# A hybrid decoder layer on one core: one block's convolution as diagonal matrices on TensorE, and the scan's scalings of x made for all chunks at once

## The chip, the core and the metric

The program runs on one core of a Trainium2 chip. The engines are named as in the profile: PE (TensorE matmul; PEld is its weight load), DVE (VectorE), ACT (ScalarE), POOL (GpSimd) and SP (SyncE, which issues most DMAs). The metric is the device time of one execution in microseconds (us): the median of three runs before the change is 1674.62 us (1671.99 to 1677.26). Everything is computed in float32 or in the matmul type fp32r; a product that has to be exact is made of three fp32r matmuls (high by high, high by low, low by high).

## The reference, cut to what matters

528 tokens (16 learned meta tokens and 512 of the sequence) with 1024 features pass one layer. The part that is touched is the mixing sub-layer:

```
u    = rmsnorm(h, norm_mix_w)
z, xbc, dt_raw, conf_in = split(u @ w_in)
# SSD group: conv of width 4, silu, then a chunked scan, 16 heads in 4 groups, chunks of 128 tokens
xdt    = xh * dt
y_diag = (C B^T * exp(segsum(dt*A))) @ xdt          # inside a chunk
states = B^T @ (decay * xdt)                        # carried from chunk to chunk
y      = y_diag + C @ prev_state * exp(cumsum) + D * xh
y      = rmsnorm_per_group(y * silu(z)) * ssd_norm_w
# Conformer group: GLU, causal depthwise conv of width 31, LayerNorm over 1024 channels, swish
g      = a * sigmoid(gate)                          # 1024 channels
hc[t]  = sum_j g[t + j - 30] * conv_w[j] + conv_b   # each channel by itself
yc     = silu(layernorm(hc) * ln_g + ln_b)
h      = h + concat(y, yc) @ w_out                  # 2048 x 1024
```

After it comes the channel sub-layer (a product-key retrieval over 128 x 128 experts) and a last RMSNorm; the change leaves them alone.

## The kernel before, in words

The mixing stage takes the first quarter of the span. Weights come in blocks of 1 MB: SP loads the raw block into one of two slots (`wload`, L167), ACT copies it to the matmul type (L184) and writes its negative (L185), and POOL issues a DMA that adds the raw block from HBM onto it (L186), which leaves the low part. High and low parts have two slots as well, so the split of a block waits until TensorE has read the last of the block two before it. `mm3` (L159 to L162) makes the three matmuls of a product.

ORDER lists the projections: `z` blocks (gate of the SSD), `x` blocks (its inputs, B and C) and `c0` to `c7`, the eight blocks of 128 channels of the Conformer group. `c_block` (L406) projects, makes the GLU on DVE (L415, L416) into `gl`, [128 channels x 542 tokens], and convolves: one ACT instruction for tap 0 (L420) and 30 DVE instructions (L422), each `o = gl[:, j:j+512] * w[j] + o` over 512 tokens. Then the block's sums for the LayerNorm are collected (L424 to L439); for `c7` they stay apart and are added by the matmuls at L676.

`ssd(g)` (L511) does one group of four heads: for each of five chunks, `prepare` scales x by dt (L528), by the decay (L530) and by D (L534), with 256 columns in each instruction, and `finish` does the matmuls with the state and makes y in a buffer of its own (L571 to L577); y of groups 0 to 2 goes to HBM and comes back. `y_split` (L616) transposes y on TensorE (L620) and splits it on ACT and DVE (L626, L627).

`out_part` is the output projection. It has eight weight blocks, here w0 to w7, two for each part: `out_part([0])` takes w0 and w1 and uses y of groups 0 and 1, `out_part([1])` w2 and w3 with groups 2 and 3, `out_part([2, 3])` w4 to w7 with the Conformer half. Each block has 48 matmuls of 128x512 and each half ends with additions into the residual on DVE (L653). Between them lies the LayerNorm (L672 to L696): the sums by matmuls (L676), a short chain on DVE and POOL (L678 to L686), the mean and the factor spread to rows by TensorE (`to_rows`, L402), then for each of eight blocks two DVE instructions (L691, L692), a Silu and a copy on ACT (L693, L695) and a subtraction on DVE (L696). Its results overwrite the places where y of groups 0 to 3 lay.

Each engine's order is fixed when the program is built: a scheduler takes instructions by priority. `late(LOWP)` puts a convolution behind, `early(SSDP)`, `early(LNP)` and `early(YP)` put the scan, the LayerNorm and the output projection ahead. An engine works through its instructions in that order.

Of the kernel before, what the change touches and what calls it, by code (L numbers as in the profile page):

```python
# [44 lines left out]
YP = 300  # L45
MO = (0, 1, -1, 2, 3)
# [19 lines left out]
def pack(inputs):  # L66
# [9 lines left out]
    for k in range(8):  # L76
# [21 lines left out]
    return dict(x=ac(g["x"][0]), meta=ac(g["meta_tokens"]), win=win, wzdt=wzdt, wout=wout, wq=wq,  # L98
                keysT=keysT, wdT=wdT, wd=ac(wd), wu=ac(wu), small=ac(small), rowb=ac(rowb), nw=ac(nw),
# [18 lines left out]
def body(ctx, tc, I, out):  # L118
# [205 lines left out]
    ybs = [mem(S0 + 3840 + 256 * k, 256) for k in range(3)]  # L324
# [5 lines left out]
    xdts = [mem(W0 + 4608 + 256 * k, 256) for k in range(3)]  # L330
    xws = [mem(W0 + 5376 + 256 * k, 256) for k in range(3)]
    YL = [mem(o, 256) for o in (S0 + 4608, S0 + 4864, F0 + 3728, F0 + 3984)]
# [73 lines left out]
    def c_block(k):  # L406
# [11 lines left out]
        cw = cwh[:, 31 * k:31 * k + 31]  # L418
        with late(LOWP):
# [5 lines left out]
            if k == 0:  # L425
                p = ps()
                for t in range(4):
                    E.matmul(p[:, t:t + 1], o[:, 128 * t:128 * t + 128], ones[:, 0:1], start=True, stop=True)
                V.tensor_scalar(ccol, p[:, 0:4], 1.0 / 128, None, op0=OP.mult)
                S.activation(crow, to_rows(ccol), AF.Copy)  # L430
                V.tensor_tensor(o, o, crow, op=OP.subtract)
                S.activation(sumq, o, AF.Square)
            else:
                at = atmp[atn[0] % 2]
                atn[0] += 1
                S.activation(at, o, AF.Square)
                if k < 7:
                    V.tensor_tensor(sumq, sumq, at, op=OP.add)
                    V.tensor_tensor(sumd, convo[:, 0, :] if k == 1 else sumd, o, op=OP.add)  # L439
                else:  # L440
                    sq7.append(at)
# [69 lines left out]
    def ssd(g):  # L511
# [5 lines left out]
        def heads(c, np_=128):  # L517
            hs = slice(16 * c + 4 * g, 16 * c + 4 * g + 4)
            return lambda a: a[:np_, hs, None].to_broadcast([np_, 4, 64])

        def prepare(c):
            np_ = NM if c == 0 else 128
            hb = heads(c, np_)
            n = rot[0]
            rot[0] += 1
            xc = XS[g % 2][:np_, c, :]
            xdt, xw = xdts[n % 3], xws[n % 3]
            V.tensor_tensor(h4(xdt[:np_]), h4(xc), hb(dtv), op=OP.mult)  # L528
            if c < 4:
                V.tensor_tensor(h4(xw[:np_]), h4(xdt[:np_]), hb(wst), op=OP.mult)  # L530
            em = pa = pe = None
            if c > 0:
                t0 = 128 * (c - 1)
                V.tensor_tensor(h4(xc), h4(xc), rowb[:, 32 + 4 * g:36 + 4 * g, None].to_broadcast([128, 4, 64]), op=OP.mult)  # L534
# [17 lines left out]
        def finish(c):  # L552
# [16 lines left out]
            if c > 0:  # L569
                y_ = ybs[n % 3] if g < 3 else YL[c - 1]  # L570
# [6 lines left out]
                S.activation(y_, y_, AF.Copy, scale=rs)  # L577
                if g < 3:
                    load(yD[c - 1, :, 256 * g:256 * g + 256], y_)
# [75 lines left out]
    with early(YP):  # L655
# [11 lines left out]
        for t in range(4):  # L667
            y_split(YL[t], t, 3, 1)
# [3 lines left out]
    with early(LNP):  # L672
# [15 lines left out]
        prs = to_rows(rst)  # L688
        for k in range(8):
# [375 lines left out]
ARRAYS = ["x", "meta", "win", "wzdt", "wout", "wq", "keysT", "wdT", "wd", "wu", "small", "rowb", "nw", "cst"]  # L1065
# [15 lines left out]
```

## Time and profile before

| | us |
|---|---|
| median of three runs | 1674.62 |
| the profiled execution | 1675.73 |
| its span, first to last instruction | 1674.0 |
| PE busy | 1620.4 (97%) |
| DVE busy | 1395.3 (83%) |
| ACT busy | 769.5 (46%) |
| POOL busy | 390.2 (23%) |

The page divides the span into 40 slices of 41.85 us and gives a digit for the busy share of each. A profiled row names line, engine, operation, output and inputs; times are from the span's start. Matmuls overlap, so the time of a matmul is taken from the distance of starts, not from its duration. The last columns of a timeline row, in brackets, are the idle time of the engine just before it and what ended it.

### The profile page before, as it was taken

Reading aid. Unit: us, or ns where it says so; the run is one execution under the profiler, and the core shown is the slowest. Engines: PE = TensorE matmul, PEld = TensorE weight load, DVE = VectorE, ACT = ScalarE, POOL = GpSimd, SP = SyncE. Lnnn points to the kernel's source line nnn. Section 1 sums busy time; section 2 is a strip of 40 time slices with the busy share of each in tenths; the row PEclk is TensorE's granted clock in tenths of the full one; section 3 lists DMA queues with packets and bytes.
Section 4 is the critical chain, followed back from the end, with each engine's and each line's share of the span. In section 5 each row is a group of like instructions: output and inputs, shape, how many; then the busy total and the mean of one; then the engine's idle time right before and its main releaser. Section 6 shows DMA issues by size and latency. Waiting matters only on the chain. (4 is left out here: it accounts for less than half of the span.)

```text
span 1674.0 us, 26115 instructions
## 1 busy us (share of the span) xinstructions
PE 1620.4 (97%) x9529; PEld 1471.2 (88%) x9529; DVE 1395.3 (83%) x2864; ACT 769.5 (46%) x1155; POOL 390.2 (23%) x336
## 2 busy tenths in 40 slices
PE   7999999887899999999999999999999999999997
PEld 7999999666788999999999988888888899999996
DVE  5999899994478998999998478888888888888876
ACT  5566566535423344567676333333333333333333
POOL 1111111000000002012233232222222355464430
PEclk9999999987999999999999999999999999999999
DMA  7877576654322356699999889999999899999982
GB/s 219 192 170 167 127 161 162 197 133 101 106 82 100 125 188 230 206 329 342 329 326 322 298 289 360 357 334 359 342 344 349 303 343 353 357 351 368 340 311 97
DMA packets 165185, 425.38 MB, mean 254 GB/s; under 512 B 14384, under 2 KB 81200, under 8 KB 159424
## 3 DMA queue, kind: packets, MB, share of 16 engines
q1 hardware_dynamic: 121568, 261.17, 44.8%
q0 software_dynamic: 43488, 162.55, 31.9%
q8 instruction: 74, 1.21, 0.3%
q14 instruction: 55, 0.45, 0.1%
HBM read 381.72 MB, written 41.94 MB: 253 GB/s over the span
## 5 line engine op out<-in xcount | busy, mean ns | idle before, releaser
L160 PE MATMUL pa<-MR 128*128 128x512 f32 (+3 forms) x2120 | 727.5, 344 | 13.8 <-ACT MR L695 7.6
L161 PE MATMUL pa<-MR 128*128 128x512 f32 (+3 forms) x2120 | 726.7, 343 | 1.0 <-DMA MR<-wout 1.0
L162 PE MATMUL pa<-MR 128*128 128x512 f32 (+3 forms) x2120 | 687.6, 343 | 1.1 <-DVE MR L267 1.0
L160 PEld LDWEIGHTS pa<-MR 128*128 128x128 f32 x2120 | 402.5, 190 | 45.1 <-ACT MR L695 7.9
L161 PEld LDWEIGHTS pa<-MR 128*128 128x128 f32 x2120 | 401.9, 190 | 31.1 <-DMA MR<-wout 1.4
L162 PEld LDWEIGHTS pa<-MR 128*128 128x128 f32 x2120 | 400.9, 189 | 32.0 <-DVE MR L267 1.2
L773 ACT ACTIVATE MR<-M 128x1024 fp32r<-128x1024 f32 (+1 forms) x264 | 285.9, 1084 | 297.9 <-PE pa L161 104.9
L774 DVE TENSOR_TENSOR MR<-M,MR 128x1024 fp32r<-128x1024 f32 (+1 forms) x264 | 330.2, 1252 | 77.2 <-ACT MR L773 71.6
L914 POOL DMA_INDIRECT M<-wd,M x128 | 160.0, 1250 | 548.8 <-DVE M L930 283.2
L914 POOL DMA_INDIRECT M<-wu,M x128 | 168.3, 1315 | 308.8 <-DVE M L937 264.3
L161 PE MATMUL pb<-MR 128*128 128x384 f32 (+1 forms) x576 | 206.8, 359 | 0.0
L160 PE MATMUL pb<-MR 128*128 128x384 f32 (+1 forms) x576 | 206.3, 359 | 0.0
L162 PE MATMUL pb<-MR 128*128 128x384 f32 (+1 forms) x576 | 204.2, 359 | 0.0
L1001 ACT ACTIVATE MR<-M 128x384 fp32r<-128x384 f32 x128 | 67.0, 523 | 274.8 <-issue 203.5
L422 DVE SCALAR_TENSOR_TENSOR M<-M 128x512 f32<-128x512 f32 x240 | 173.7, 746 | 3.9 <-ACT M L420 3.0
L937 DVE SCALAR_TENSOR_TENSOR M<-M 128x1024 f32<-128x1024 f32 x128 | 163.7, 1279 | 15.6 <-DMA M<-wu,M 15.3
L930 DVE SCALAR_TENSOR_TENSOR M<-M 128x1024 f32<-128x1024 f32 x128 | 154.1, 1219 | 10.1 <-DMA M<-wd,M 10.0
L1002 DVE TENSOR_TENSOR MR<-M,MR 128x384 fp32r<-128x384 f32 x128 | 71.2, 556 | 59.9 <-ACT MR L1001 59.2
L161 PEld LDWEIGHTS pb<-MR 128*128 128x128 f32 x576 | 108.1, 188 | 11.3
L160 PEld LDWEIGHTS pb<-MR 128*128 128x128 f32 x576 | 108.1, 188 | 11.3
L162 PEld LDWEIGHTS pb<-MR 128*128 128x128 f32 x576 | 108.1, 188 | 10.8
L976 ACT ACTIVATE M<-pb 128x512 f32<-128x512 f32 x96 | 98.9, 1159 | 37.5 <-PE pb L974 37.5
(221 smaller groups left out, 1469.5 us busy)
## 6 DMA issues: line engine op xcount, KB each, us to landing
M<-wdT SPq DMA_DIRECT2D x128, 512.0 KB
M<-wu SPq DMA_DIRECT2D x128, 512.0 KB
GD<-M SPq DMA_DIRECT2D x40, 512.0 KB
M<-GD SPq DMA_DIRECT2D x32, 640.0 KB
M<-win SPq DMA_DIRECT2D x19, 1024.0 KB
MR<-win POOLq DMA_DIRECT2D x38, 512.0 KB
HD<-M SPq DMA_DIRECT2D x88, 192.0 KB
M<-HD SPq DMA_DIRECT2D x88, 192.0 KB
```

The source lines that it names most:

```text
L160: E.matmul(o, lh, rh, start=first, stop=False)
L161: E.matmul(o, lh, rl, start=False, stop=False)
L162: E.matmul(o, ll, rh, start=False, stop=last)
L422: V.scalar_tensor_tensor(o, gl[:, j:j + 512], cw[:, j:j + 1], o, op0=OP.mult, op1=OP.add)
L773: S.activation(wh, raw, AF.Copy)
L774: leng.tensor_tensor(wl, raw, wh.bitcast(F32), op=OP.subtract)
L914: r = G.indirect_dma_start(out=g, out_offset=None, in_=src, in_offset=bass.IndirectOffsetOnAxis(ap=e3[:, k:k + 1], axis=0))
L930: use(V.scalar_tensor_tensor(g, g, 1.0, x2s, op0=OP.mult, op1=OP.mult, accum_out=dots[:, k:k + 1]))
L937: use(V.scalar_tensor_tensor(h1[3], g, act3[:, k:k + 1], h1[3], op0=OP.mult, op1=OP.add))
L976: S.activation(gb.rearrange("p i t -> p t i")[:, c:c + 4, :], p.rearrange("p (t i) -> p t i", t=4), AF.Copy, scale=1.0 / GS)
L1001: S.activation(sh, sf, AF.Copy)
L1002: V.tensor_tensor(sl, sf, sh.bitcast(F32), op=OP.subtract)
```

## The change

Three things are changed.

1. Block `c7` has no DVE convolution any more. `c_diag` splits `gl` into a high and a low part (L270, L271 of the changed kernel), loads 31 diagonal matrices of 128x128 (a new input, `cdiag`, two blocks of 1 MB that go the way of all weights), and adds 31 products of three matmuls of 128x512 into one PSUM tile. ACT then adds the bias (L460), DVE subtracts the offset (L461) and ACT squares (L463).
2. The scalings of x are made at the head of `ssd(g)` for all chunks of the group: one instruction of 1280 columns and two of 1024 (L548) in place of 13 of 256. The scaled copies have one buffer instead of three in turn, and y takes the place of x, from where it is stored or, for group 3, transposed.
3. In the LayerNorm the DVE instructions are pinned to program order, with the subtraction for block k two blocks later (L722).

```diff
+DGP = 0
+    cdiag = np.zeros((2, 128, 16, 128), np.float32)
+    for j in range(31):
+        cdiag[j // 16, np.arange(128), j % 16, np.arange(128)] = g["conf_conv_w"][0].reshape(31, 1024)[j, 896:]
...
-    ybs = [mem(S0 + 3840 + 256 * k, 256) for k in range(3)]
+    ybs = [mem(o, 256) for o in (S0 + 4864, W0 + 5888, F0 + 3728, F0 + 3984)]
...
-    xdts = [mem(W0 + 4608 + 256 * k, 256) for k in range(3)]
-    xws = [mem(W0 + 5376 + 256 * k, 256) for k in range(3)]
+    xdta = mem(W0 + 4608, 1280).rearrange("p (c n) -> p c n", c=5)
+    xwa = mem(S0 + 3840, 1024).rearrange("p (c n) -> p c n", c=4)
...
         cw = cwh[:, 31 * k:31 * k + 31]
+        if k == 7:
+            c_diag(gl, o)
+            return
...
+    def c_diag(gl, o):
+        gh, gw = memr(16960, 544)[:, 0:542], memr(17504, 544)[:, 0:542]
+        split_to(gh, gw, gl[:, 0:542])
+        p = ps("pa")
+        for q in range(2):
+            src = I["cdiag"][q].rearrange("p j n -> p (j n)")
+            wh, wl = wsplit(wload(src), src, parts=2)
+            for j in range(16 - q):
+                ds = slice(128 * j, 128 * j + 128)
+                t0 = 16 * q + j
+                mm3(p, wh[:, ds], wl[:, ds], gh[:, t0:t0 + 512], gw[:, t0:t0 + 512], t0 == 0, t0 == 30)
+        with early(DGP):
+            S.activation(o, p, AF.Identity, scale=0.5, bias=small[:, S_CB + 7:S_CB + 8])
+            V.tensor_tensor(o, o, crow, op=OP.subtract)
+            at = atmp[atn[0] % 2]
+            S.activation(at, o, AF.Square)
+            sq7.append(at)
...
+        scaled(xdta, xs, by_chunk(dtv, 5), 5)
+        scaled(xwa, xdta[:, 0:4], by_chunk(wst, 4), 4)
+        scaled(xs[:, 1:5], xs[:, 1:5], rowb[:, None, 32 + 4 * g:36 + 4 * g, None], 4)
...
-            V.tensor_tensor(h4(xdt[:np_]), h4(xc), hb(dtv), op=OP.mult)
-            if c < 4:
-                V.tensor_tensor(h4(xw[:np_]), h4(xdt[:np_]), hb(wst), op=OP.mult)
...
-                V.scalar_tensor_tensor(y_, y_, 0.5, ZB[g % 2][:, c - 1, :], op0=OP.mult, op1=OP.mult)
-                S.activation(xdt, y_, AF.Square, accum_out=ss[:, c - 1:c])
+                V.scalar_tensor_tensor(xc, y_, 0.5, ZB[g % 2][:, c - 1, :], op0=OP.mult, op1=OP.mult)
+                S.activation(xdt, xc, AF.Square, accum_out=ss[:, c - 1:c])
...
+        def low(k):
+            ch, cl = hl(k)
+            pin(V.tensor_tensor(cl, convo[:, k, :], ch.bitcast(F32), op=OP.subtract))
+
         for k in range(8):
             cv = convo[:, k, :]
-            V.tensor_tensor(cv, cv, prs, op=OP.mult)
-            V.tensor_tensor(cv, cv, prh, op=OP.subtract)
+            pin(V.tensor_tensor(cv, cv, prs, op=OP.mult))
+            pin(V.tensor_tensor(cv, cv, prh, op=OP.subtract))
             S.activation(cv, cv, AF.Silu, bias=small[:, S_LB + k:S_LB + k + 1], scale=small[:, S_LG + k:S_LG + k + 1])
-            ch, cl = hl(k)
-            S.activation(ch, cv, AF.Copy)
-            V.tensor_tensor(cl, cv, ch.bitcast(F32), op=OP.subtract)
+            S.activation(hl(k)[0], cv, AF.Copy)
+            if k > 1:
+                low(k - 2)
```

The new functions move the line numbers: L184 and L185 become L188 and L189, L402 becomes L407, L422 L430, L436 L444, L620 L649, L626 L655, L653 L682, L676 L705, L691 to L696 L722 to L729.

The order that the scheduler writes changes around the LayerNorm. On PE, before, the sums stand at the end of `out_part([1])`: the last rows are the sums of `c7` and the spreading (pb_3898 is the PSUM tile of the sums, pa_3841 one of `out_part([1])`, pa_3973 one of `out_part([2, 3])`).

```order
L161 MATMUL pa_3841<-MR_64 128x512
L162 MATMUL pa_3841<-MR_64 128x512
L676 MATMUL pb_3898<-M_63 128x1 x8
L402 MATMUL pb_3922<-M_63 128x128 x4
L402 MATMUL pb_3927<-M_63 128x128 x4
L160 MATMUL pa_3973<-MR_64 128x512
L161 MATMUL pa_3973<-MR_64 128x512
```

In the changed kernel they stand in the middle of `out_part([0])`: pa_3461 is the convolution of `c7`, whose last six matmuls come after the first half of `out_part([0])` (pa_3643 is its last tile); pa_3700 to pa_3703 are the tiles of its second half.

```order
L166 MATMUL pa_3461<-MR_64 128x512
L705 MATMUL pb_3940<-M_63 128x1 x8
L164 MATMUL pa_3700<-MR_64 128x512
L164 MATMUL pa_3701<-MR_64 128x512
L164 MATMUL pa_3702<-MR_64 128x512
L164 MATMUL pa_3703<-MR_64 128x512
L705 MATMUL pb_3940<-M_63 128x1 x8
L407 MATMUL pb_3964<-M_63 128x128 x4
L407 MATMUL pb_3969<-M_63 128x128 x4
L165 MATMUL pa_3700<-MR_64 128x512
```

So 192 matmuls of the output projection follow the LayerNorm's sums before, and 332 after: 44 of `out_part([0])`, 96 of `out_part([1])` and the same 192.

On ACT, before, the squares of the last two convolutions (L436) stand ahead of the split of w5 and the Silus.

```order
L184 ACTIVATE MR_64<-M_63 128x2048
L185 ACTIVATE MR_64<-MR_64 128x2048
L436 ACTIVATE M_63<-M_63 128x512 x2
L184 ACTIVATE MR_64<-M_63 128x2048
L185 ACTIVATE MR_64<-MR_64 128x2048
L693 ACT_TABLE_LOAD
L693 ACTIVATE M_63<-M_63 128x512 x2
```

In the changed kernel the splits of two weight blocks, w1 and w2, stand around the end of the convolution (L460 reads its PSUM tile, L463 squares).

```order
L188 ACTIVATE MR_64<-M_63 128x2048
L444 ACTIVATE M_63<-M_63 128x512
L188 ACTIVATE MR_64<-M_63 128x2048
L460 ACTIVATE M_63<-pa_3461,M_63 128x512
L189 ACTIVATE MR_64<-MR_64 128x2048 x2
L463 ACTIVATE M_63<-M_63 128x512
L728 ACT_TABLE_LOAD
L728 ACTIVATE M_63<-M_63 128x512 x3
```

The first L188 is that of w1, whose slot the second block of diagonals held; the second is that of w2, whose slot w0 held.

## Rows read from the trace of the kernel before

**Rows 1.** The page: the span in 40 slices, busy tenths of PE and DVE, and from the list of waits of PE the two largest (line, released by; us in total, times, longest).

```profile
PE   7999999887899999999999999999999999999997
DVE  5999899994478998999998478888888888888876
...
PE pa L620 <- DVE MR L627: 9.6, 5, 4.7
PE pa L160 <- ACT MR L695: 7.6, 1, 7.6
```

**Rows 2.** Windows of 25 us around the end of the mixing stage: length, busy time of PE, PEld, DVE, ACT, POOL with instruction counts, granted TensorE clock (1.00 is 2.4 GHz), DMA share, GB/s.

```profile
275.00:300.00 25.00, 23.37 (x189) 22.12 (x188) 22.76 (x51) 14.52 (x30) 3.12 (x4) 1.00 0.66 198
300.00:325.00 25.00, 19.24 (x100) 15.65 (x100) 24.09 (x57) 11.97 (x35) 1.55 (x2) 0.86 0.62 182
325.00:350.00 25.00, 18.25 (x85) 14.19 (x83) 25.00 (x53) 14.96 (x29) 3.47 (x5) 0.89 0.63 154
350.00:375.00 25.00, 23.98 (x106) 20.00 (x107) 24.41 (x41) 5.39 (x6) 0.90 (x1) 0.90 0.41 106
375.00:400.00 25.00, 14.88 (x66) 12.74 (x65) 15.29 (x30) 15.08 (x20) 1.95 (x2) 0.66 0.40 98
```

**Rows 3.** The timeline of DVE: start, length, line and operation; two instructions in a row, the last GLU of the projections, the tail of the convolutions, and the LayerNorm.

```profile
270.31 0.42 DVE L572 TENSOR_TENSOR M<-M 128x256 f32<-128x256 f32 x1
270.65 0.74 DVE L422 SCALAR_TENSOR_TENSOR M<-M 128x512 f32<-128x512 f32 x1
...
298.11 0.44 DVE L415 SCALAR_TENSOR_TENSOR M<-M,pa 128x272 f32<-128x272 f32 x1 [0.66 <-PE pa L162]
...
342.82 0.86 DVE L627 SCALAR_TENSOR_TENSOR MR<-pa,M,MR 128x128 fp32r<-128x128 f32 x3
...
352.98 4.72 DVE L422 SCALAR_TENSOR_TENSOR M<-M 128x512 f32<-128x512 f32 x7
...
373.79 0.69 DVE L424 TENSOR_TENSOR M<-M 128x512 f32<-128x512 f32 x1
...
378.43 0.17 DVE L678 TENSOR_SCALAR M<-pb 128x8 f32<-128x8 f32 x1 [0.99 <-PE pb L676]
...
384.67 4.87 DVE L691 TENSOR_TENSOR M<-M,pb 128x512 f32<-128x512 f32 x8 [3.94 <-PE pb L402]
```

**Rows 4.** The timeline of PE: the first wait for a stored y, the end of the projections, the waits after it, one chunk of the scan, the LayerNorm, the last four weight blocks (first row L160 at 392.26) and what follows them (L611).

```profile
296.99 0.44 PE L620 MATMUL pa<-M 128*128 128x128 f32 x2 [1.63 <-DMA M<-yD]
...
306.42 1.09 PE L620 MATMUL pa<-M 128*128 128x128 f32 x4 [4.68 <-DVE MR L627]
...
316.70 0.70 PE L559 MATMUL pb<-M 128*128 128x256 f32 x2 [0.44 <-DVE M L549]
...
318.07 0.65 PE L563 MATMUL pb<-M 128*128 128x256 f32 x2
...
339.54 0.82 PE L620 MATMUL pa<-M 128*128 128x128 f32 x6
...
351.02 0.80 PE L160 MATMUL pa<-MR 128*128 128x512 f32 x1 [2.53 <-DVE MR L627]
...
376.55 1.84 PE L676 MATMUL pb<-M 128*128 128x1 f32 x16
...
380.88 3.75 PE L402 MATMUL pb<-M 128*128 128x128 f32 x16 [2.48 <-DVE M L686]
392.26 0.79 PE L160 MATMUL pa<-MR 128*128 128x512 f32 x1 [7.63 <-ACT MR L695]
417.24 0.50 PE L161 MATMUL pa<-MR 128*128 128x512 f32 x1 [0.98 <-DMA MR<-wout]
...
438.92 1.91 PE L611 MATMUL pb<-M 128*128 128x128 f32 x16
```

**Rows 5.** The timeline of ACT and of POOL: the split of w6.

```profile
405.19 1.92 ACT L184 ACTIVATE MR<-M 128x2048 fp32r<-128x2048 f32 x1 [5.09 <-PE pa L162]
407.13 1.92 ACT L185 ACTIVATE MR<-MR 128x2048 fp32r<-128x2048 f32 x1
...
409.35 0.86 POOL L186 DMA_DIRECT2D MR<-wout  x1 [27.53 <-ACT MR L185]
```

**Rows 6.** Windows of 4 us of PE: length, busy time, granted clock, DMA share, GB/s.

```profile
304.00:308.00 4.00, 1.58 (x8) 0.50 1.08 277
...
392.00:396.00 4.00, 3.74 (x9) 0.51 0.00 0
396.00:400.00 4.00, 4.00 (x19) 1.00 0.00 0
...
408.00:412.00 4.00, 4.00 (x19) 1.00 1.00 295
```

**Rows 7.** Groups of ACT from 250 to 440 us, shapes apart: line, operation, shapes, count, busy us, mean ns, idle time before them and what ended it.

```profile
L626 ACT ACTIVATE MR<-pa,M 128x128 fp32r<-128x128 f32 x32 | 10.3, 370 | 11.1 <-PE pa L620 8.0 <-DVE MR L627 2.9
...
L693 ACT ACTIVATE M<-M 128x512 f32<-128x512 f32 x8 | 6.1, 800 | 8.3 <-DVE M L692 8.3
L695 ACT ACTIVATE MR<-M 128x512 fp32r<-128x512 f32 x8 | 4.6, 615 | 0.0
...
L436 ACT ACTIVATE M<-M 128x512 f32<-128x512 f32 x4 | 2.5, 624 | 7.4 <-DVE M L424 7.4
```

**Rows 8.** A group of DVE up to 440 us, shapes apart, columns as in rows 7: a convolution tap.

```profile
L422 DVE SCALAR_TENSOR_TENSOR M<-M 128x512 f32<-128x512 f32 x240 | 173.7, 746 | 3.9 <-ACT M L420 3.0
```

More of the change, by code (lines that the diff above doesn't have):

```diff
@@ L98, in pack @@
     return dict(x=ac(g["x"][0]), meta=ac(g["meta_tokens"]), win=win, wzdt=wzdt, wout=wout, wq=wq,
-                keysT=keysT, wdT=wdT, wd=ac(wd), wu=ac(wu), small=ac(small), rowb=ac(rowb), nw=ac(nw),
+                keysT=keysT, wdT=wdT, wd=ac(wd), wu=ac(wu), small=ac(small), rowb=ac(rowb), nw=ac(nw), cdiag=cdiag,
                 cst=consts_array())
@@ L323, in body @@
     EM = [mem(S0 + 2304 + 512 * k, 512) for k in range(3)]
-    ybs = [mem(S0 + 3840 + 256 * k, 256) for k in range(3)]
+    ybs = [mem(o, 256) for o in (S0 + 4864, W0 + 5888, F0 + 3728, F0 + 3984)]
+    for xs_ in XS:
+        V.memset(xs_[:, 0, :], 0.0)
     padb = [mem(A0 + 2304 + 532 * k, 532) for k in range(2)]
@@ L436, in c_block @@
                 S.activation(at, o, AF.Square)
[L437 to L441, printed above, removed]
+                V.tensor_tensor(sumq, sumq, at, op=OP.add)
+                V.tensor_tensor(sumd, convo[:, 0, :] if k == 1 else sumd, o, op=OP.add)
+    def c_diag(gl, o):
[15 more added lines that the diff above has]
+            sq7.append(at)
     sm = con(80 * 12)
@@ L515, in ssd, with heads, scaled @@
         ready = {}
[L517 removed]
+        xs = XS[g % 2]
+        def heads(c):
             hs = slice(16 * c + 4 * g, 16 * c + 4 * g + 4)
[L519 removed]
+            return lambda a: a[:, hs, None].to_broadcast([128, 4, 64])
+        def scaled(dst, src, col, n):
+            c4 = lambda a: a.rearrange("p c (h d) -> p c h d", h=4)
+            V.tensor_tensor(c4(dst), c4(src), col.to_broadcast([128, n, 4, 64]), op=OP.mult)
+        by_chunk = lambda a, n: a.rearrange("p (c h) -> p c h", c=5)[:, 0:n, 4 * g:4 * g + 4, None]
+        scaled(xdta, xs, by_chunk(dtv, 5), 5)
+        scaled(xwa, xdta[:, 0:4], by_chunk(wst, 4), 4)
+        scaled(xs[:, 1:5], xs[:, 1:5], rowb[:, None, 32 + 4 * g:36 + 4 * g, None], 4)
         def prepare(c):
             np_ = NM if c == 0 else 128
[L523 removed]
             n = rot[0]
             rot[0] += 1
[L526 to L530 removed]
+            xc, xdt = xs[:, c, :], xdta[:, c, :]
+            xw = xwa[:, c, :] if c < 4 else None
             em = pa = pe = None
@@ L569, in finish @@
             if c > 0:
-                y_ = ybs[n % 3] if g < 3 else YL[c - 1]
+                y_ = ybs[n % 4]
                 V.tensor_tensor(h4(y_), h4(pa[:, 128:384]), hb(eacs), op=OP.mult)
@@ L573, in finish @@
                 V.tensor_tensor(y_, y_, pd[:, 0:256], op=OP.add)
-                V.scalar_tensor_tensor(y_, y_, 0.5, ZB[g % 2][:, c - 1, :], op0=OP.mult, op1=OP.mult)
-                S.activation(xdt, y_, AF.Square, accum_out=ss[:, c - 1:c])
+                V.scalar_tensor_tensor(xc, y_, 0.5, ZB[g % 2][:, c - 1, :], op0=OP.mult, op1=OP.mult)
+                S.activation(xdt, xc, AF.Square, accum_out=ss[:, c - 1:c])
                 rs = rstd_of(ss[:, c - 1:c], 1, 1.0 / 256)
-                S.activation(y_, y_, AF.Copy, scale=rs)
+                S.activation(xc, xc, AF.Copy, scale=rs)
                 if g < 3:
-                    load(yD[c - 1, :, 256 * g:256 * g + 256], y_)
+                    load(yD[c - 1, :, 256 * g:256 * g + 256], xc)
         prepare(0)
@@ L667, in body @@
         for t in range(4):
-            y_split(YL[t], t, 3, 1)
+            y_split(XS[1][:, t + 1, :], t, 3, 1)
         out_part([1])
@@ L1062, in body @@
         final(m)
-ARRAYS = ["x", "meta", "win", "wzdt", "wout", "wq", "keysT", "wdT", "wd", "wu", "small", "rowb", "nw", "cst"]
+ARRAYS = ["x", "meta", "win", "wzdt", "wout", "wq", "keysT", "wdT", "wd", "wu", "small", "rowb", "nw", "cdiag", "cst"]
 def kernel(**inputs):
```

5 lines of the change are left out of this document (3 added, 2 removed).

## The prediction

> **What bounds the kernel now.** I read the slices of the page first. PE has the digit 9 in nearly all of them, but slices 8 to 11 (300 to 460 us) fall to 7 or 8, and DVE is full there [rows 1]. The change works in just that stretch. Up to 296 us PE is full with projections, so what DVE saves there is worth nothing. In the windows of 25 us DVE then shows 24.1, 25.0 and 24.4 of 25 us from 300 to 375 while PE has gaps, and from 375 to 400 PE has only 14.9 [rows 2]. The timeline of DVE tells why: the convolutions of c6 and c7 are put behind everything else, run on without a break, and end at 373.79 + 0.69 = 374.5 [rows 3]. Only then can the LayerNorm's sums be closed; its first large instruction starts at 384.67 [rows 3], and PE waits 7.63 us for its first result until 392.26 [rows 4]. The last four weight blocks then take until 438.92, where the next stage begins [rows 4]. So the stage ends by a chain: convolutions on DVE, 10.2 us of LayerNorm start, 7.6 us to the first result, 46.7 us of matmuls. I predict how far the time 438.92 moves; what follows does not change and moves with it.
>
> **What goes from DVE.** Thirty taps. A tap lasts 746 ns [rows 8], but seven in a row take 4.72 us [rows 3], so the next starts every 0.66 us: 30 x 0.66 = 19.9 us. The new order also puts 16 of the 32 split instructions (L627: three in 0.86, so 0.26 each) and 11 of the 15 additions (L653, 0.60 each by the eight of L691 in 4.87) behind the LayerNorm [rows 3]: 10.8 us more. From the last GLU at 298.11 to 374.5 DVE works without a real break, so the convolutions could be done near 374.5 - 31 = 344.
>
> **The scalings of x.** Thirteen instructions of 256 columns go for three long ones in each group; the count of columns stays, so only the fixed part of an instruction is saved. A 256-column one of the scan is followed 0.34 us later by the next (270.31, 270.65), a 512-column one 0.60 us later (L691) [rows 3]: the fixed part is 2 x 0.34 - 0.60 = 0.08. Taken from a lone instruction's 0.42 instead it would be 0.15, and if the long ones hide it no better it is nothing. I take 0.08: ten instructions x 4 groups x 0.08 = 3 us of DVE, between 0 and 6. For three groups it falls before 296 us, under PE. For group 3 the two long ones stand between the halves of the last GLU and hold it back by 2.3 us; this is in the sum below. y in the place of x moves no time that I can see: its stores and loads are the same.
>
> **What comes to PE.** 93 matmuls of 128x512. The last four blocks are 4 x 48 = 192 matmuls between 392.26 and 438.92; without the wait of 0.98 [rows 4] and 2 us for the start at 0.51 of the clock (the 1.2 GHz level, for some 4 us [rows 6]) that is 43.7 us, 0.228 us each. So 21.2 us are added. The page "TensorE: Matmul & The Clock Gate" of the Trainium skill (section "Wait — 56ns, not 53.3ns?") gives 215.7 ns for such a matmul at full clock; by it the 93 would cost 20.1 and the sum would be 1.1 us lower. This trace shows 0.228 for such a run in which the weights change at two of three matmuls, and I keep that.
>
> **The chain of the changed kernel**, on the time scale of the profile before, by the new order.
> 1. Projections end at 295.7: before they end at 298.2, and the wait of 1.63 at 296.99 [rows 4] and two transposed pairs (0.4 each) now come later.
> 2. The convolution's matmuls begin at 303. The last GLU on DVE with the two long scalings (2.3), three taps (2.0) and the low part (0.6) ends at 301.3, and a pair of transposes ahead of most of the matmuls wants a y whose load stands behind a 1 MB weight load. Before, PE waited at the same place, 4.68 us until 306.42 [rows 4].
> 3. They end at 344.7. Up to there PE does the 93 and the 48 of w0, without the first three 138 x 0.228 = 31.5; three chunks of the scan at 1.7 (316.70 to some 318.4 [rows 4]), two preparations at 0.7 and five pairs of transposes at 0.4, 8.2 together; and 2 us for a start at half clock, as at 304 to 308 [rows 6]. DVE is done with c6 before that, so it is PE that decides.
> 4. The LayerNorm's first large instruction: 361.5. ACT has in its queue, in this order, the copy of w1 (its slot is free when the last diagonal is read), the square of c6, the copy of w2, the evacuation of c7's sum, the two negatives and the square of c7: four times 1.92 [rows 5] and three times 0.62 [rows 7], 9.5 us, until 354.2. The sums on PE take 1. From L678 to L691 were 6.24 us (378.43 to 384.67 [rows 3]). Before, this stretch took 10.2 us from the end of the taps; here it takes 16.8.
> 5. The other 44 matmuls of the first part want the low part of w1. Its DMA is issued at 354.3 behind that of w2 and two raw loads. A lone one lands 7.0 us after the issue (410.2 to 417.24 [rows 4, 5]); at 295 GB/s with the DMA engines full [rows 6] some 2.6 MB are still ahead, so 362.5. 44 x 0.228 + 2 for the half clock: 374.5.
> 6. Then the y of groups 2 and 3. PE's order puts its transposes and out_part([1]) behind those 44. ACT first splits w3 (2 x 1.92), and does 16 splits at 0.29 (0.37 less the overlap), three Silus and a copy [rows 5, 7], about 11.5 us in one queue: 386 (the Silu's 0.80 and the copy's 0.62 likewise less the overlap). Before, eight such y took from 339.54 to 351.02, the same 11.5 [rows 4].
> 7. Six weight blocks remain, w2 to w7. w2 takes 10.9 and 2 for the half clock, to 398.9; w3 to 409.8. A later block is ready 12.05 us after the end of the one two before it (405.19 to 417.24 [rows 4, 5]), and takes 10.9: w4 to 421.9, w5 (ACT has a Silu and copies ahead, 0.7) to 433.5, w6 to 444.9, w7 to 456.5.
>
> So the stage ends at 456.5 where it ended at 438.92: 17.6 us later. LayerNorm starts 23 us earlier, but 332 matmuls follow it instead of 192 (140 x 0.228 = 31.9), and PE stands still at two places where before it stood at one. The profiled execution took 1675.73; 1675.7 + 17.6 = 1693.3. The median of the runs shown is 1.1 us below that execution, so **1692 us**. The extra loads of cdiag (4 MB, of 425) fall where the DMA engines are busy 0.62 to 0.66 of the time [rows 2], and I give them no cost; if the second one came late, step 2 or 3 would grow by up to the 7 us of one landing. The pinned order of the LayerNorm I give no cost, since out_part([1]) covers it.
>
> **Rivals.**
> *PE is not held up (faster).* The place is PE between 344.7 and the end. If DVE were all that held the stage, the waits at steps 4 to 7 would close, and PE's own work would set the end: 344.7 + 5.6 (the sums 1.84 and the spreading 3.75, L676 and L402 [rows 4]) + 332 x 0.228 = 75.7 + 3.4 for the transposes + 2 = 431.4, 7.5 us earlier than before: 1675.7 - 7.5 - 1.1 = 1667. For it: DVE is full and PE has gaps exactly here [rows 2]. Against it: the copies of w1 and w2 stand ahead of the evacuation in ACT's own order. My steps hold 25 us of breaks (13 at the LayerNorm, 8 at y, 4 and more at weights and clock); the point that decides is 7.5 us of them.
> *The two cancel (no change).* The transposes of y hide and weights come without a wait, but the LayerNorm's break stays: 374.5 + 3.4 + 6 x 10.9 = 443, 4 us later, 1678. For it speaks that in the first part the same splits ran beside matmuls.
> *It gets worse.* The diagonals come late (7 us, above), or the clock falls again at each of the five stops (2 us each, two more than I count): 27 us, 1702.
> *The scalings count.* All 6 us of the bound on the path would give 1686; but they lie under PE, so I only widen by it.
>
> **How the numbers follow.** My forecast, 1684 to 1700, has a chance of 0.50; a smaller loss, 1680 to 1684, 0.10; the worse case 0.12; no change 0.11; faster 0.17. 0.3% is 5 us, about what a measurement can tell: slower by more than that 0.72, within it 0.11, faster 0.17. The range that holds 8 in 10 reaches from the faster case to the worse one, 1667 to 1703; the forecast's own is 1684 to 1700.
>
> **What would show it.** Right: no taps of c7 on DVE and 93 matmuls of pa with cdiag; DVE waiting in the stretch 345 to 410; an ACT copy of 2048 columns between the last matmul of c7's sum and its evacuation; PE idle some 13 us around the sums and some 8 before out_part([1]); the transposes after out_part, L640 (L611 before), starting near 456. Wrong: L640 before 439, or the LayerNorm's first row before 350. If PE is busy without a stop from 345 on, the first rival holds.

## The result, and the profile after

The changed kernel takes 1696.0 us, the median of four runs (1695.6 to 1701.4), beside 1674.6 (1672.0 to 1677.3) for the kernel before in the same session. The ratio is 1.0136, with a 95% interval of 1.0123 to 1.0148: slower by 21.4 us. The forecast was 1692, with 0.72 on slower.

The profiled execution of the changed kernel is the longest of the four, 1701.4 us with a span of 1699.6. Lengths read from it can be some microseconds above the usual ones; the comparison between kernels below goes by medians.

The page of the changed kernel, first its busy times and then the slices of PE and DVE that answer to [rows 1]:

```profile
PE 1646.4 (97%) x9622; PEld 1491.6 (88%) x9622; DVE 1377.8 (81%) x2797; ACT 778.2 (46%) x1164; POOL 393.7 (23%) x340
...
PE   7999999877999999999999999999999999999997
...
DVE  5999899744259999999999458888888789888876
```

DVE lost 17.5 us of work and has the digits 7, 4, 4 and 2 in the slices 8 to 11. PE gained 26.0, and in the slices 8 to 10 it still has 8, 7 and 7. What DVE gave up did not close the gaps of PE. The windows of 25 us, columns as in [rows 2], say where they are now:

```profile
300.00:325.00 25.00, 17.49 (x81) 14.20 (x80) 16.26 (x37) 6.40 (x23) 0.66 (x1) 0.80 0.43 127
325.00:350.00 25.00, 25.00 (x124) 20.68 (x123) 22.93 (x48) 10.18 (x21) 3.47 (x4) 1.00 0.47 137
350.00:375.00 25.00, 16.11 (x66) 13.51 (x65) 6.63 (x15) 11.36 (x10) 2.78 (x3) 0.60 0.72 189
375.00:400.00 25.00, 16.65 (x66) 12.97 (x64) 15.46 (x34) 14.20 (x27) 0.92 (x1) 0.79 0.35 85
400.00:425.00 25.00, 24.41 (x108) 19.87 (x107) 9.02 (x14) 10.68 (x9) 1.72 (x2) 1.00 0.46 123
```

From 325 to 350 PE is full, with the matmuls of the convolution and of w0. From 300 to 325 and from 350 to 400 neither PE nor DVE is full: the stage now waits along a chain that goes through several engines. The timeline of PE, columns as in [rows 4], shows the stops of that chain; the first matmul of the next stage (L640, L611 before) is its end:

```profile
308.29 0.66 PE L649 MATMUL pa<-M 128*128 128x128 f32 x2 [7.51 <-DMA M<-yD]
...
358.50 1.87 PE L705 MATMUL pb<-M 128*128 128x1 f32 x8 [1.52 <-ACT M L463]
...
362.85 3.75 PE L407 MATMUL pb<-M 128*128 128x128 f32 x16 [2.48 <-DVE M L715]
...
370.60 0.80 PE L165 MATMUL pa<-MR 128*128 128x512 f32 x1 [4.00 <-DMA MR<-wout]
...
385.41 0.44 PE L649 MATMUL pa<-M 128*128 128x128 f32 x2 [1.70 <-DVE M L682]
...
391.38 2.07 PE L649 MATMUL pa<-M 128*128 128x128 f32 x8 [5.54 <-DVE MR L656]
...
394.56 0.79 PE L164 MATMUL pa<-MR 128*128 128x512 f32 x1 [1.11 <-DVE MR L656]
...
465.11 1.91 PE L640 MATMUL pb<-M 128*128 128x128 f32 x16
```

The stage ends at 465.1; before, it ended at 438.92 [rows 4]. The 26.2 us between them are the 25.6 by which the two spans differ (1699.6 and 1674.0), so nothing behind this stage counts.

Two stops stand out. At 308.29 a pair of transposes waits 7.5 us for a y that SP issued at 297.76, behind a weight block of 1 MB; before, PE waited 4.68 at this place [rows 4] (that row names a split on DVE; in that trace the load of the y landed at 306.3, too). The timeline of SP (start, length of the issue, what is loaded):

```profile
297.33 0.33 SPq L158 DMA_DIRECT2D M<-wout  x1
297.76 0.80 SPq L158 DMA_DIRECT2D M<-yD  x1
```

And at the end of the convolution ACT has the queue that the prediction described, but for the names of the two blocks (below). The timelines of ACT and of POOL, where L188 and L189 split the two weight blocks, L460 evacuates the sum, L463 squares it, and L190 issues the low parts:

```profile
349.52 1.92 ACT L188 ACTIVATE MR<-M 128x2048 fp32r<-128x2048 f32 x1 [4.51 <-PE pa L166]
351.34 0.61 ACT L444 ACTIVATE M<-M 128x512 f32<-128x512 f32 x1
351.86 1.89 ACT L188 ACTIVATE MR<-M 128x2048 fp32r<-128x2048 f32 x1
353.66 0.67 ACT L460 ACTIVATE M<-pa,M 128x512 f32<-128x512 f32 x1
354.23 3.70 ACT L189 ACTIVATE MR<-MR 128x2048 fp32r<-128x2048 f32 x2
357.83 0.62 ACT L463 ACTIVATE M<-M 128x512 f32<-128x512 f32 x1
```

```profile
356.43 0.89 POOL L190 DMA_DIRECT2D MR<-wout  x1 [11.96 <-ACT MR L189]
358.23 0.86 POOL L190 DMA_DIRECT2D MR<-wout  x1 [0.91 <-ACT MR L189]
```

The timeline of PE at that place; three rows out of a run of 512-column matmuls, of which the last six belong to the convolution:

```profile
349.10 0.39 PE L166 MATMUL pa<-MR 128*128 128x512 f32 x1
349.32 0.40 PE L164 MATMUL pa<-MR 128*128 128x512 f32 x1
...
350.50 0.39 PE L166 MATMUL pa<-MR 128*128 128x512 f32 x1
```

ACT had been idle for 4.51 us when the first copy began at 349.52. It had waited for the matmul at 349.10, the last that reads w0, so this copy is that of w2, which takes w0's slot. The section on the change and the prediction call it the copy of w1. That cannot be, since the last six matmuls of the convolution, from 349.32 to 350.50, still read the diagonals whose slot w1 takes. The copy of w1 is the second, at 351.86. The low parts go in the same order, that of w2 at 356.43 and that of w1 at 358.23; the low part of w1 was there at 370.6.

### The profile page after: what moved, and what is told of

It reads as the page before. It is cut to its first block, busy times and chain, and to the rows that moved or that the text cites. A ratio compares the mean times of both kernels' runs of the same rounds, so it can differ in the third digit from the quotient of the medians.

```text
span 1699.6 us, 26271 instructions
## 1 busy us (share of the span) xinstructions
PE 1646.4 (97%) x9622; PEld 1491.6 (88%) x9622; DVE 1377.8 (81%) x2797; ACT 778.2 (46%) x1164; POOL 393.7 (23%) x340
## 5 line engine op out<-in xcount | busy, mean ns | idle before, releaser
L165 PE MATMUL pa<-MR 128*128 128x512 f32 (+3 forms) x2151 | 742.0, 345 | 5.7 <-DMA MR<-wout 5.7
L164 PE MATMUL pa<-MR 128*128 128x512 f32 (+3 forms) x2151 | 739.6, 345 | 4.7 <-ACT M L833 1.4
L166 PE MATMUL pa<-MR 128*128 128x512 f32 (+3 forms) x2151 | 702.1, 345 | 1.2 <-DVE MR L271 1.1
L165 PEld LDWEIGHTS pa<-MR 128*128 128x128 f32 x2151 | 409.2, 190 | 39.1 <-DMA MR<-wout 7.7
L164 PEld LDWEIGHTS pa<-MR 128*128 128x128 f32 x2151 | 408.6, 190 | 37.2 <-ACT MR L270 1.9
L166 PEld LDWEIGHTS pa<-MR 128*128 128x128 f32 x2151 | 408.2, 190 | 33.5 <-DVE MR L271 1.3
L974 DVE SCALAR_TENSOR_TENSOR M<-M 128x1024 f32<-128x1024 f32 x128 | 163.8, 1280 | 16.9 <-DMA M<-wu,M 16.6
L430 DVE SCALAR_TENSOR_TENSOR M<-M 128x512 f32<-128x512 f32 x210 | 152.3, 747 | 2.3 <-ACT M L428 1.1
L166 PEld LDWEIGHTS pb<-MR 128*128 128x128 f32 x576 | 108.1, 188 | 10.8
```

The costliest lines, as they stand in the source:

```text
L164: E.matmul(o, lh, rh, start=first, stop=False)
L165: E.matmul(o, lh, rl, start=False, stop=False)
L166: E.matmul(o, ll, rh, start=False, stop=last)
L430: V.scalar_tensor_tensor(o, gl[:, j:j + 512], cw[:, j:j + 1], o, op0=OP.mult, op1=OP.add)
L974: use(V.scalar_tensor_tensor(h1[3], g, act3[:, k:k + 1], h1[3], op0=OP.mult, op1=OP.add))
```

## The experiments

Three theories were set against each other. **A**: what costs is the order in which work stands on PE and ACT around the convolution and the LayerNorm. **B**: PE is the bound throughout, and 93 matmuls at 0.228 us are simply 21.2 us. **C**: the scan's part, with its single buffers and y in x's place, carries the loss.

The table gives for each kernel the median, the ratio to the kernel before with its interval, and from one profiled execution the length from 296 us to the first matmul of the next stage with PE's busy time in it (the window view over exactly that stretch); idle is their difference. Between executions the point 296 itself lies up to 1.6 us earlier or later in the work, so lengths are good to about that.

| kernel | us | ratio | from 296 us to the end | PE busy | PE idle |
|---|---|---|---|---|---|
| before | 1674.6 | | 142.9 | 117.3 | 25.6 |
| the change | 1696.0 | 1.0136 [1.0123, 1.0148] | 169.1 | 142.1 | 27.0 |
| diagonals alone | 1690.3 | 1.0102 [1.0085, 1.0119] | 157.2 | 136.1 | 21.1 |
| scan's part alone | 1678.6 | 1.0029 [1.0006, 1.0052] | 143.0 | 119.0 | 24.0 |
| LayerNorm's order alone | 1669.2 | 0.9969 [0.9957, 0.9982] | 137.5 | 118.0 | 19.5 |
| diagonals and LayerNorm | 1685.1 | 1.0061 [1.0040, 1.0081] | 155.6 | 137.2 | 18.4 |
| one product of three | 1660.4 | 0.9917 [0.9900, 0.9933] | 129.2 | 118.9 | 10.3 |
| two products of three | 1673.5 | 0.9987 [0.9973, 1.0001] | 145.9 | 130.4 | 15.5 |
| convolution first of all | 1693.3 | 1.0109 [1.0084, 1.0133] | 164.5 | 140.8 | 23.7 |
| sums behind | 1695.9 | 1.0120 [1.0095, 1.0145] | 164.6 | 136.8 | 27.8 |
| diagonals first | 1689.3 | 1.0090 [1.0073, 1.0107] | 157.4 | 136.3 | 21.1 |
| y's pair later | 1680.4 | 1.0037 [1.0026, 1.0048] | 147.6 | 134.7 | 12.9 |

In the changed kernel the stage is 26.2 us longer than before, 24.8 of PE's busy time and 1.4 of idle time: the added matmuls stand there in full, and the waits of before have been exchanged for others of the same length. What the experiments have to tell is whether that could have been otherwise.

### Each of the three parts alone

The edits are the matching parts of the diff above, put into the kernel before.

> The kernel before with part 1 alone: c7's convolution on TensorE, the scan and the LayerNorm as before. Theory A (the convolution's matmuls stand on PE's path ahead of the LayerNorm, and what is behind it waits in PE's and ACT's order): 8 to 16 us slower than before, since 288 matmuls of the output projection now follow the LayerNorm's sums. Theory B (PE is the bound everywhere, so 93 x 0.228 us are simply added): 21 us slower. Theory C (the scan's single buffers and y in the place of x carry the loss): within 4 us of before.

> The kernel before with part 2 alone: the scalings for all chunks at once, y in the place of x. Theories A and B: within 4 us of before, since PE is full until 296 and 3 us of DVE are all that is saved. Theory C: 12 us or more slower, by a wait of PE for a stored y or of DVE for the single buffer.

> The kernel before with part 3 alone: the LayerNorm's DVE instructions block by block instead of eight and eight. All theories leave it near before; by the chain read from before it should be 3 to 6 us faster, since the first Silu need not wait for eight instructions (PE's wait of 7.63 at 392.26 shrinks to about 3). If it is slower by 5 or more, the pinned order has a part in the loss.

Measured: +16.3 us for the diagonals (beside a median of 1674.0 for the kernel before in that session), between 1 and 9 for the scan's part by its interval, and -4.8 for the LayerNorm. C falls as a cost of its own: with the scan's part alone the stage has its length of before (in an execution of 1675.6; where the 1 to 9 us of the median come from is not shown). The diagonals cost a little more than A's 8 to 16 and less than B's 21.2. The pinned order, which the prediction gave no effect, is worth 4.8 us. The sum of the three is 11.5 plus 1 to 9, and the whole change cost 21.4.

### Fewer products

```diff
-                mm3(p, wh[:, ds], wl[:, ds], gh[:, t0:t0 + 512], gw[:, t0:t0 + 512], t0 == 0, t0 == 30)
+                E.matmul(p, wh[:, ds], gh[:, t0:t0 + 512], start=t0 == 0, stop=t0 == 30)
```

> The changed kernel with one of the three matmuls of each tap (high by high), 31 instead of 93; it leaves out the low parts of c7's convolution. Theory B: 62 x 0.228 = 14 us faster than the changed kernel, about 1682. Theory A: more than that, 18 to 28 us faster, 1668 to 1678, since the order then closes the LayerNorm's sums behind all of out_part([0]) and its chain no longer stands open on PE. Theory C: within 5 us of the changed kernel.

The second kernel keeps two products:

```diff
-                mm3(p, wh[:, ds], wl[:, ds], gh[:, t0:t0 + 512], gw[:, t0:t0 + 512], t0 == 0, t0 == 30)
+                E.matmul(p, wh[:, ds], gh[:, t0:t0 + 512], start=t0 == 0, stop=False)
+                E.matmul(p, wh[:, ds], gw[:, t0:t0 + 512], start=False, stop=t0 == 30)
```

> The changed kernel with two of the three products of the convolution's matmuls, 62 and not 93; it leaves out the low part of the diagonals. The planner's order is that of the changed kernel up to the convolution's end, and then that with one product: all of out_part([0]) ahead of the LayerNorm, 288 matmuls behind it. With three products 1696.0 and with one 1660.4 were measured. B (every matmul costs 0.228 us and nothing else): 7 us faster than three, 1689. A (the order behind the convolution is the larger part): 7 to 12 us slower than one product, 1667 to 1673. In proportion, with no jump: 1678.

From three products to two the time fell by 22.5 us, from two to one by 13.1; 31 matmuls are 7.1 us each time. So the matmuls' own time explains less than a third of the first step, and 1660.4 is below even A's 1668 to 1678. In both kernels the planner puts all of the convolution ahead of the output projection, and all of `out_part([0])` ahead of the LayerNorm's sums. With one product the wait at the y pair is 2.8 us in place of 7.5, since 18 matmuls now stand ahead of the pair. B falls as the whole account of what the matmuls cost. The kernel with one product is faster than the kernel before, by 13.6 us, but it is another computation: the low parts of `c7`'s input and weights are left out.

### The diagonals with the LayerNorm's order

The edit is the diff above without its second part.

> The kernel before with the diagonals and the LayerNorm's pinned order, without the scan's part. With the diagonals alone 1690.3 was measured, with the pin alone 4.8 us less than before. Additive: 1685.5. A (the pin gains where DVE is full, and with the diagonals DVE is not): 1688 to 1692. C (the scan's part is what takes the changed kernel from there to 1696): this comes out 4 us or more under the changed kernel, under 1692, where its pin and diagonals are the same.

1685.1: the two effects add up (+16.3 and -4.8 would be 1685.5). The expectation that the pin gains nothing once DVE has room was wrong. The scan's part, worth at most 9 us alone and nothing in the stage, takes the kernel from here to 1696.0, as C had it for this kernel. PE's order shows what changes with it. With the diagonals and the LayerNorm one matmul of `out_part([0])` stands ahead of the convolution's last; in the changed kernel 48 do, and the convolution's last six come behind them (the order that the section on the change shows). With another order written into the changed kernel (below, 1689.3) 6.7 of these 10.9 us come back; the other 4.2 are not told apart.

### The LayerNorm's sums behind `out_part([0])`

```diff
         p = ps()
-        for c0, src in ((0, sumd), (4, sumq), (8, convo[:, 7, :]), (12, sq7[0])):
-            for t in range(4):
-                E.matmul(p[:, c0 + t:c0 + t + 1], src[:, 128 * t:128 * t + 128], ones[:, 0:1], start=True, stop=True)
+        with tc.issue_after(ends[0].ins):
+            for c0, src in ((0, sumd), (4, sumq), (8, convo[:, 7, :]), (12, sq7[0])):
+                for t in range(4):
+                    E.matmul(p[:, c0 + t:c0 + t + 1], src[:, 128 * t:128 * t + 128], ones[:, 0:1], start=True, stop=True)
```

`ends[0]` is the last matmul of `out_part([0])`.

> The changed kernel, whole in what it computes, with one order written in: the LayerNorm's sums are issued on PE behind all 96 matmuls of out_part([0]), so that 288 matmuls follow them as in the kernel with the diagonals and the pinned LayerNorm alone (1685.1). Up to the convolution's end PE's order is the changed kernel's, with its wait of 7.5 us for the third pair's y. If the order behind the convolution is what the changed kernel loses against that one: 1684 to 1690, and the wait of 4.0 us for the low part of w1 shrinks to 2 to 3 us, ahead of the sums. If the scan's part costs in another way (its single buffers, the y in x's place): 1693 to 1698. Whatever of the 15.7 us that the later pair gave is left then belongs to the wait at the pair: 5 to 10 us.

1695.9: nothing gained, and this reading of A fell. How many matmuls stand behind the LayerNorm, 288 or 332, does not decide. PE's timeline in this kernel tells what does:

```profile
352.60 1.34 PE L164 MATMUL pa<-MR 128*128 128x512 f32 x4 [2.92 <-ACT MR L188]
368.17 0.80 PE L165 MATMUL pa<-MR 128*128 128x512 f32 x1 [14.23 <-DMA MR<-wout]
```

The sums and the spreading no longer stand in between, and PE waits 14.2 us for the low part of w1, which comes at 368.2 here (an execution that runs 1.5 us ahead) and at 370.6 in the changed kernel. There the LayerNorm's break hid most of that wait, so that only 4.0 of it showed as a wait for a DMA. So the arrival of w1 sets this place, in both orders.

### The convolution's matmuls ahead of `out_part([0])`

w1 takes the slot of the second block of diagonals, which is free when the last of the 93 matmuls has read it. Two kernels move that moment. The first puts all of `c_diag` under a high priority; the body is otherwise the same:

```diff
     def c_diag(gl, o):
+        with early(400):
```

> The changed kernel, whole in what it computes, with all of c_diag in early(400): the convolution's 93 matmuls stand ahead of out_part([0]), and on ACT its evacuation and square stand ahead of the copies that split w1 and w2. A: the 7.7 us that those four copies held up the evacuation go, and the LayerNorm's first large instruction comes 8 to 14 us earlier than the 366.6 of the changed kernel; but 360 matmuls then follow the sums (336 the spreading), so of this the end keeps 2 to 8 us: 1688 to 1694. B: within 3 us of the changed kernel, 1693 to 1699. If the number of matmuls behind the LayerNorm decides by itself: 28 more than 332 by 0.228, 6 us slower, 1702.

The second only holds back the matmuls of the output projection:

```diff
+                with tc.issue_after(behind[0].ins):
                     mm3(po[t], sh[:, 128 * t:128 * t + 128], sl[:, 128 * t:128 * t + 128],
```

`behind[0]` is the last of the 93.

> The changed kernel, whole in what it computes, with one order written in: the first matmul of out_part([0]) is issued behind the last of the convolution's 93. In the changed kernel 48 matmuls of w0 stand ahead of the last six of the 93. The third pair of y's transposes stays where it is, behind the first of the 93, with its wait of 7.5 us. W (the last six hold the weight slot that w1 needs; with the LayerNorm's sums moved behind out_part([0]) PE waited 14.2 us for the low part of w1): ACT copies w1 at 336 to 341 and not at 349.5, the wait for w1's low part is under 4 us, and the time falls by 8 to 13 us, to 1683 to 1688. Then the pair's place is worth the rest of the 15.7 us that its move gave, 3 to 8. P (the move of the pair gave those 15.7 us by itself): 1692 to 1697.

The second gave 1689.3, 6.7 us of the 21.4 back, between the two forecasts. Its timeline of ACT shows the copy of w1 (L188) at 336.93 for 351.86, some 13 us earlier in the work, as the scan of this execution runs 1.6 us ahead, with the evacuation (now L463) right behind it. (The 349.5 of the expectation is the copy of w2.)

```profile
336.93 1.92 ACT L188 ACTIVATE MR<-M 128x2048 fp32r<-128x2048 f32 x1 [0.67 <-PE pa L165]
338.75 0.67 ACT L463 ACTIVATE M<-pa,M 128x512 f32<-128x512 f32 x1
```

and its timeline of PE the wait for the low part of w1, now 1.2 us, and then three waits for y's splits:

```profile
349.70 0.50 PE L165 MATMUL pa<-MR 128*128 128x512 f32 x1 [1.22 <-DMA MR<-wout]
...
373.85 0.44 PE L652 MATMUL pa<-M 128*128 128x128 f32 x2 [3.93 <-DVE MR L659]
377.28 1.54 PE L652 MATMUL pa<-M 128*128 128x128 f32 x6 [3.00 <-DVE MR L659]
...
382.68 0.80 PE L164 MATMUL pa<-MR 128*128 128x512 f32 x1 [3.86 <-DVE MR L659]
```

So the theory W of this expectation holds in what it says of the order: with the last six matmuls ahead of the 48, w1 is prepared 13 us earlier and PE hardly waits for it. In the changed kernel the copy and the transfer of w2 stand ahead of those of w1 too, and here they come later; slot and queue are not told apart. Part of the gain went into a wait that came next: the low parts of y of groups 2 and 3 on DVE, 10.8 us here and 8.4 in the changed kernel (1.70 for an addition into the residual, L682, then 5.54 and 1.11).

The first, `early(400)`, moved the same copy to 339.7 and waits no more than 0.7 us for any weights, and yet gave only 2.7 us; 1693.3 lies in the ranges of A and of B and does not tell them apart. It leaves the transposes of y group 1 in one block between the convolution and the output projection, where PE waits 1.7 for the evacuation and 4.1 for splits, and takes the sums between the first half's matmuls; 10.8 us of waits for y's splits in all. That is not told apart further.

### The y pair behind half of the convolution

```diff
+                if t0 == 15:
+                    behind.append(last)
...
-                y_split(yq[t], t, g, 1)
+                with tc.issue_after(behind[0].ins) if g == 0 and t == 2 else ExitStack():
+                    y_split(yq[t], t, g, 1)
```

> The changed kernel, whole in what it computes, with one order written in: the third pair of y's transposes is issued behind the 48th of the convolution's 93 matmuls, not behind the first. The planner then also puts all 96 matmuls of out_part([0]) ahead of the LayerNorm, so that 288 matmuls follow it and not 332. A (PE's order is what costs): the wait of 7.5 us at the pair goes, the diagonals begin 5 to 7 us earlier, and the time falls by 8 to 16 us against the changed kernel, to 1680 to 1688. B (the 93 matmuls themselves are the price, as all of them stand on a full PE): no more than 3 us, 1693 to 1697. D (the load is late whatever stands in front of it, and something else is late next): the pair waits at its new place too, and the time falls by 0 to 4 us.

1680.4: of the 21.4 us 15.6 are gone with no instruction removed. The planner's answer includes what the kernel before it here did (all 93 ahead of `out_part([0])`, some 70 of that ahead of the sums and the rest ahead of the spreading), so the pair's place itself is worth about the step from 1689.3 to 1680.4, 8.9 us, a little over the 3 to 8 that the last expectation left for it. The windows of 4 us, first of the changed kernel and then of this one (columns as above; the granted clock is the third figure from the end):

```profile
304.00:308.00 4.00, 0.00 (x0) 0.00 (x0) 0.78 (x2) 0.00 (x0) 0.00 (x0) 0.50 1.01 288
308.00:312.00 4.00, 3.71 (x10) 3.08 (x11) 2.62 (x7) 1.15 (x4) 0.00 (x0) 0.50 0.28 95
312.00:316.00 4.00, 4.00 (x15) 3.12 (x15) 2.49 (x6) 0.51 (x2) 0.00 (x0) 0.77 0.00 0
```

```profile
304.00:308.00 4.00, 4.00 (x24) 3.50 (x23) 4.00 (x10) 0.07 (x1) 0.00 (x0) 1.00 0.85 285
308.00:312.00 4.00, 4.00 (x21) 3.05 (x21) 4.00 (x10) 1.42 (x6) 0.98 (x1) 1.00 0.01 4
312.00:316.00 4.00, 4.00 (x23) 3.35 (x22) 4.00 (x8) 2.69 (x5) 0.00 (x0) 1.00 0.10 24
```

From 304 to 308 the changed kernel's PE and ACT do nothing while the DMA engines are full (1.01); the matmuls that follow run at the 1.2 GHz level. With the pair moved PE works on through the load, at 2.4 GHz, and waits only 0.9 us for the split of `gl`. D falls: at its new place the pair does not wait.

### Some of the taps by diagonals

Two kernels try a smaller dose, in the kernel before with the LayerNorm's order: 16 or 8 taps of `c7` on PE, the others on DVE, with the pair behind those matmuls.

```diff
+        for j in range(NT):
+            ds = slice(128 * j, 128 * j + 128)
+            last = mm3(p, wh[:, ds], wl[:, ds], gh[:, j:j + 512], gw[:, j:j + 512], j == 0, j == NT - 1)
+        S.activation(o, p, AF.Identity, scale=0.5, bias=small[:, S_CB + 7:S_CB + 8])
+            for j in range(NT, 31):
+                V.scalar_tensor_tensor(o, gl[:, j:j + 512], cw[:, j:j + 1], o, op0=OP.mult, op1=OP.add)
```

> The kernel before with the LayerNorm's pinned order and 16 of the 31 taps of c7 by diagonals (48 matmuls), 15 left on DVE, the third pair of y's transposes behind those matmuls; all of the result is computed, without the scan's part. PE gets 10.9 us of work, DVE loses 15 taps of 0.66 and gains one split of 0.6: 9.3 us. A (the work pays where PE would have waited for DVE): PE's idle time in the stage, 19.5 us with the pinned LayerNorm alone, falls by 10 to 16, the time is 1663 to 1669, at or under the 1669.2 of the pin alone. B (each matmul costs its 0.228 us): 1669.2 + 10.9 = 1680.

> As the one before it, with 8 of the 31 taps of c7 by diagonals (24 matmuls), 23 left on DVE. PE gets 5.5 us, DVE loses 4.0. A: 1664 to 1669. B: 1674.7.

Contrary to what the expectation says, these two do not compute the whole result: the name `NT` is also a constant of the expert stage much later (4 in all other kernels), which these two set to 16 and 8. Their times, 1719.9 and 1686.1, hold that change too and say nothing on the question. What can be read from the trace is the mixing stage, which lies ahead of it. From 296 us it takes 146.9 and 143.8 us, beside 137.5 with the LayerNorm's order alone: 9.4 and 6.3 longer, where B's price was 10.9 and 5.5. PE's idle time there is 18.0 and 20.0, beside 19.5. So A's hope that this work would fill PE's waits is not borne out. PE waits at other places instead: with 16 taps 4.64 us at 304.0 for the high part of `gl` on ACT, and 5.07 at 329.4 for an instruction of the scan on DVE. Why the scan came later was not tried.

## Why the prediction was right, and where it was off

The direction and the cause stood: DVE is relieved, PE's own work and its stops set the end. Step by step, on the changed kernel's trace:

1. Projections end: the last GLU on DVE starts at 296.0 for 295.7. Right.
2. The convolution's matmuls begin at 308.6 for 303. **This term was mis-sized, by 5.6 us.** The wait named for it, a pair of transposes whose y is loaded behind 1 MB of weights, is exactly the one that came. The prediction does not write out how 303 follows, and its only figure for this wait is the 4.68 of before [rows 4]; it was 7.51 and ended two us later than that one, at 308.29. The kernel with the pair moved, 8.9 us faster, fits its length and the clock: there the matmuls begin 6.9 us earlier in the work, and some 2.4 us more go to the 12 matmuls that start 0.43 us apart for 0.23 in the changed kernel (an estimate from its rows).
3. From there to the end of the convolution and of w0 42.1 us (to 350.7), for 41.7. Right, with the 2 us for the half clock; the terms for the scan and the transposes add up to 8.5, not the 8.2 that stand there. What the prediction counted and did not question is that the 48 of w0 lie inside: the last six of the 93 behind them hold w1's slot.
4. The LayerNorm's first large instruction at 366.6 for 361.5, 15.9 us after the end of the convolution, for 16.8. Right for its length; it is late by step 2. The prediction takes the first copy in ACT's queue for that of w1 and lets it wait for the last diagonal. It is that of w2 and waits for the last matmul of w0, 1.4 us before the convolution ends. The sum holds both copies, so no more than that hangs on the name.
5. The 44 matmuls begin at 370.6 for 362.5. The low part of w1 was issued at 358.2 for 354.3, which is 3.9 us: the end of the convolution was 6.0 late by steps 2 and 3, and ACT's queue behind it took 7.5 for 9.6. **The other 4.2 are its landing, the second term that was mis-sized**: with two of these transfers issued 1.8 us apart, it came 12.4 us after its issue; the prediction has 8.2 (and the 2.6 MB at 295 GB/s that it names would be 8.8). The 44 take 12.3 for 12.
6. y of groups 2 and 3: 11.7 us for 11.5. Right.
7. The last six blocks: 70.5 us for 70.5, to 465.1 for 456.5. Right.

So the profiled stage ended 8.6 us later than forecast: 3.9 that came through from step 2, 4.2 of landing in step 5, and small ones. The median is 4.0 above the forecast, as the profiled execution was 5.4 above the median. The prediction gave the LayerNorm's pin no effect: alone and with the diagonals it gained 4.8 and 5.2 us, which is a term that was missed. The scan's part, bounded between a gain of 6 and nothing, gained nothing. Of the signs that the prediction named, PE's idle time around the sums was 8.8 us (0.24, 0.57, 1.52, 2.48 and 4.00) for some 13, and 8.4 before out_part([1]) for some 8.

The diagonals' loads were given no cost. The kernels with the LayerNorm's order alone and with the scan's part alone, both without diagonals, also wait for that y, 4.1 us until 304.8 and 4.3 until 305.8, so a good part of that wait is not of their making. But in the changed kernel POOL issues the low part of the second block of diagonals, in two halves, at 293.97 and 298.69, around the load of this y (297.76); how far they add to the wait was not tried by itself.

Of the rivals, "the two cancel" (1678) asked that y's transposes hide and the weights come without a wait, while the LayerNorm's break stays. With one pair moved the time was 1680.4, near it, but by another way: there PE has no wait at the LayerNorm, and still waits 8.4 us for y's splits and 3.3 for weights. So breaks can close, but by the order, and the change's own order did not close them. The faster rival (1667) asked for a PE without stops; with 93 matmuls the least idle time seen was 12.9 us. What stays of the loss with the better order is 6 us by the medians; in the table's lengths PE is busy 17.4 us longer there than before (21.2 of matmuls, less what the clock gave, 0.94 over that stretch for 0.88) and idle 12.7 less.

The version that beats both kernels with the whole result is the LayerNorm's order alone: 1669.2, 0.9969 of before.

## What to carry to other kernels

PE takes its matmuls in the order written, so a wait for a small load costs what stands behind it: before work is moved to PE, look for the first instruction in its order that waits, and put the new, independent work ahead of it, not behind. Where buffers turn in two slots, the last instruction that reads a slot sets when the next block's preparation starts; with six matmuls left behind 48 others a weight block was prepared some 13 us later. And taking work from a full engine pays only as far as the other engine's idle time closes, which is read from the stage, as length, busy and idle, for each version.

## What the runs showed of the hardware

- PE keeps to its order. In the changed kernel 92 matmuls of the convolution stood behind the waiting pair for 7.5 us; with the pair moved they began at 300.4 (in an execution that runs 1.4 us ahead). The Trainium skill says so ("PSUM — Partial Sum Buffer", section "Engine vs sequencer instructions": matmuls start and complete in program order), and this trace agrees.
- With those 7.5 us without work the granted clock fell to 0.50, the 1.2 GHz level, from 304 to 312, and matmuls of 512 columns started 0.43 us apart, for 0.23 at 1.00. With the pair moved it did not fall there.
- A load of 128 KB took 10.5 us from its issue (297.76) to the instruction that waited for it (308.29), while the DMA engines were full (a share of 1.01 from 304 to 308): a weight block of 1 MB was issued 0.43 us before it, and the low part of the diagonals at 293.97 and 298.69.
- A wait can hide behind another. The DMA wait for w1 showed as 4.0 us in the changed kernel and as 14.2 when the LayerNorm's sums were taken out of its way, with no change in the time.
